# Odd attention in a two-model Trainium2 kernel: a head's scores by turns with the last head's transposes

## The chip, the cores and the metric

The kernel runs on one core of one Trainium2 chip. The metric is the device time of one execution in microseconds (us). Engines are named as the profile names them: PE is TensorE (its weight loads are PEld), DVE is VectorE, ACT is ScalarE, POOL is GpSimd, SP is SyncE. L194 is line 194 of the kernel before.

## The reference, cut to what matters

Two models run one after the other on 512 tokens of width 1024. The first has two layers of mixing and a feed-forward block. The second has an even layer and an odd layer, each with attention and a SwiGLU block. The change is in the odd layer's attention, and to a small part in the even layer's window attention. All arithmetic is float32; each operand of a large product is split into a high and a low part, and three products stand for one.

```python
def _odd_mixer(h, hc, w_in, w_out, q_g, k_g, rel_bias, ctx_out):
    q, k, v = split(h @ w_in)            # 16 heads of 64, q and k with an RMS norm
    qc, kc, vc = split(hc @ w_in)        # the same of 256 context tokens
    o = _neighbourhood_attention(q, k, v, kc, vc, rel_bias) @ w_out

def one_row(r):                          # of _neighbourhood_attention
    s_nb = jnp.einsum('bqhd,bjhd->bhqj', q_row, k_rows) * scale + bias[None]
    s_nb = jnp.where(mask[None, None], s_nb, NEG_2)
    s_cx = jnp.einsum('bqhd,bjhd->bhqj', q_row, k_ctx) * scale
    p = jax.nn.softmax(jnp.concatenate([s_nb, s_cx], axis=-1), axis=-1)
    return (jnp.einsum('bhqj,bjhd->bqhd', p[..., :n], v_rows)
            + jnp.einsum('bhqj,bjhd->bqhd', p[..., n:], v_ctx))
```

## The kernel before

One Python program writes straight-line code, with no loops left on the chip. A planner of the tile framework then lays down each engine's queue: it takes the instruction of highest priority, which is the one that the program wrote first, among those that its own costs hold ready and for whose output a buffer is free.

Odd attention (`odd`, L1403) handles its 16 heads in 4 groups of 4. `proj` (L1413) is the projection of one group to keys, queries and values. It is a generator: each step issues three matmuls of 256 columns and says what they take by the code's own count (0.33 us). `later` (L129) puts such a generator into a queue, `fill(us)` (L132) takes steps of it until `us` are used up, `drain` takes all the rest. During group `gr` the queue holds the projection of the next group, 128 steps or 42.2 us; during the last it holds three quarters of the out projection (`out_part`, L1437), 48 steps of 0.65 or 31.2 us. It ends each row block with a gate addition on DVE (`gate_add`, L1104).

A head has two stages. `s1` (L1483) loads the head's relative bias in three DMAs, subtracts it from the mask on POOL (L1492, L1494), and for each of 4 query blocks makes the scores (recorded as L438 and L439), adds the mask and takes the minimum on DVE (L443), and takes the exponential on ACT (L1508, L1514, L1516), whose running sums are added and inverted by DVE (L1520, L1521). A fill of 0.85 us follows each block. `s2` (L1524) calls `window_av` (L1022), which goes through 5 groups of blocks: PE transposes the exponentials into PSUM (L1030 for the two context groups, L1039 for the three window groups), ACT casts the high half and DVE subtracts for the low half (`split_r` and `split`, L176 and L177), a fill of 0.85 follows, and then PE adds the product with the values to `po` (L1034, L1048). At the end `fold` (L487) brings `po` to the output slab of the pair of heads, and one more fill follows.

The heads of a group go by `s1(1)`, `s2(0)`, `s1(2)`, `s2(1)` and so on: all four score blocks of a head, then all five groups of the head before. At the first head of each pair `stacks` (L1473) transposes queries and keys (L391) and writes them, scaled, to slabs (`stack`, L394: L407 on ACT, L411 and L413 on DVE). At the end of a pair `over_sums` (L495) spreads the 8 reciprocals of a token to 512 columns on POOL (L500), transposes that on PE (L504), multiplies on DVE (L506), and the pair's output is split for the out projection (`cat`).

Weights come by DMA into 4 raw buffers; ACT and DVE split them (`weight`, L164 and L165). Slabs of 2 KB per partition come from two pools in this stage, `F` with 18 and `R` with 23 slabs. Of PSUM's 8 banks 4 have the tag `A` (scores, transposes, `po`) and 4 the tag `G` (projections).

Of the kernel before, what the change touches and what calls it, by code (L numbers as in the profile page):

```python
# [10 lines left out]
F32R = mybir.dt.float32r  # L11
BF = mybir.dt.bfloat16
AF = mybir.ActivationFunctionType
# [27 lines left out]
OF = (0.85, 0.85, 0.85)  # L41
# [6 lines left out]
ODD = dict(F=18, R=23, L=4)  # L48
# [6 lines left out]
class Gen:  # L55
# [28 lines left out]
    def F(self, name, n=512):  # L84
        return self.tile("F", name, [128, 512])[:, :n]

    def R(self, name, n=512):
        return self.tile("R", name, [128, 512], F32R)[:, :n]
# [406 lines left out]
    def over_sums(self, y, rc, ident, view=None):  # L495

# [4 lines left out]
                                   rc.rearrange("p i e -> p (i e)")[:, :, None].to_broadcast([128, 2 * n, 64]))  # L501
        ps = self.P()[:, :n * 128]
# [519 lines left out]
    def window_av(self, es, ident, fill, vst, vctx):  # L1022
# [3 lines left out]
        hl, where = [], {}  # L1026
        for cb in range(2):
# [7 lines left out]
        for b, blocks in enumerate(self.WP):  # L1035
# [7 lines left out]
            self.fill(fill)  # L1043
            for kb in sorted({k for k, _ in blocks}):
                qs = [i for k, i in blocks if k == kb]
                o = blocks.index((kb, qs[0])) * 128
                for a, p in enumerate((h, l)):
                    nc.tensor.matmul(po[:, qs[0] * 128:qs[-1] * 128 + 128], vst[kb], p[:, o:o + len(qs) * 128],  # L1048
                                     start=False, stop=(b == 2 and a == 1))
        return po  # L1050
# [200 lines left out]
    def even(self, sc, sx, y):  # L1251
# [48 lines left out]
        def heads(z, scale, new, s1, s2, cat):  # L1300
            qs, ya, rc, prev = {}, {}, {}, None
            for h in range(9):
# [8 lines left out]
                if prev is not None:  # L1311
                    j = (h - 1) // 2
                    s2(h - 1, prev, ya[j])
                    if h % 2 == 0:
                        self.over_sums(ya[j], rc[j], self.ident)
# [45 lines left out]
        def s2(h, es, ya):  # L1361
            g = h // 4
            po = self.window_av(es, self.ident, EF[1], [v[:, g] for v in vst], [v[:, g] for v in vc])
            self.fold(ya, po, h % 2)
            self.fill(EF[2])
# [37 lines left out]
    def odd(self, sc, st):  # L1403
# [59 lines left out]

        new = lambda: ([], [], [])
        nxt = new()
        self.drain(proj(0, *nxt))
        for gr in range(4):
            zq, zk, vx = nxt
            nxt = new()
            self.later(proj(gr + 1, *nxt) if gr < 3 else out_part())  # L1470
            st_ = {}

            def stacks(hp):  # L1473
                qt = self.heads_t(zq, hp * 128, self.rident)
                q2 = [self.stack(qt, e, False, gcol[:, 0:1]) for e in range(2)]
                kt_ = self.heads_t(zk[2:], hp * 128)
                k2 = [self.stack(kt_, e, True, gcol[:, 1:2]) for e in range(2)]
                kt_ = self.heads_t(zk[:2], hp * 128)
                c2 = [self.stack(kt_, e, True, gcol[:, 1:2]) for e in range(2)]
                for e in range(2):  # L1480
                    st_[hp * 2 + e] = q2[e], k2[e], c2[e]

            def s1(hl, rc):  # L1483
                h = gr * 4 + hl
                qs, kx, kc = st_[hl]
                bias = self.small("nab", [128, 3, 256], bufs=2)
                src = t["od_rel_bias_2"][h]
                for v in range(3):
                    self.load(bias[:, v, :249], bass.AP(tensor=src.tensor, offset=src.offset + (16, 8, 0)[v],
# [330 lines left out]
```

## Time and profile before

| what | value |
|---|---|
| time, median of 3 runs | 3478.66 us (3477.15 to 3480.24) |
| the profiled execution's own time | 3484.61 us |
| its span, from the first to the last instruction | 3482.8 us |
| mean granted clock of PE | 0.993 |
| busy share of the span: PE, PEld, DVE, ACT, POOL | 98%, 84%, 63%, 45%, 8% |
| HBM traffic | 385.05 MB read, 16.88 MB written |

The profile shows one execution. A row of a group of instructions gives line, engine, operation, output and inputs, shapes, count, then busy time and mean duration, then the engine's idle time before them and what ended it. PE's matmuls overlap, so a single one's duration is longer than the step to the next. Odd attention's projection of the first group starts at about 2734 us, its heads run from 2776 to 3091 us, in four groups that begin near 2776, 2858, 2942 and 3024 us.

### The profile page before, as it was taken

How to read it: one execution, taken by the hardware profiler on the slowest of the kernel's cores; microseconds unless marked ns; L12 is line 12 of the kernel's file. 1: busy time of each engine (PE TensorE's matmuls, PEld its weight loads, DVE VectorE, ACT ScalarE, POOL GpSimd, SP SyncE). 2: the span in 40 equal slices, each digit the busy share in tenths (PEclk: the TensorE clock that was granted, in tenths of full speed). 3: DMA queues.
4: the chain of work that ended last, by engine and by line, in shares of the span. 5: the costliest groups of instructions: out<-in, count | busy, mean ns of one | idle time of the engine just before them, and what ended most of it. 6: DMA issues, size and time to landing. Idle time of an engine off the chain costs nothing.

```text
span 3482.8 us, 48256 instructions
## 1 busy us (share of the span) xinstructions
PE 3403.7 (98%) x18462; PEld 2938.1 (84%) x18462; DVE 2191.0 (63%) x3822; ACT 1560.6 (45%) x2933; POOL 276.4 (8%) x525
## 2 busy tenths in 40 slices
PE   9999999999999999999999999999999999989999
PEld 8888888888888888888887889888888888878887
DVE  5567646999564765579857777673334566673433
ACT  5545434424464553343434567553223466652222
POOL 2200000000031000000001100000000333300000
PEclk9999999999999999999999999999999999999999
DMA  4231234665323212446733133453333333233322
GB/s 127 84 91 55 76 106 153 204 220 176 111 76 107 67 61 85 144 151 218 252 121 129 61 121 126 145 189 121 97 97 120 81 57 62 66 110 112 97 91 85
DMA packets 144790, 405.06 MB, mean 116 GB/s; under 512 B 26768, under 2 KB 34992, under 8 KB 144560
## 3 DMA queue, kind: packets, MB, share of 16 engines
q1 hardware_dynamic: 144560, 401.99, 37.1%
q8 instruction: 145, 2.38, 0.3%
q14 instruction: 85, 0.70, 0.1%
HBM read 385.05 MB, written 16.88 MB: 115 GB/s over the span
## 4 chain that ended last, share of the span: by engine, by line
PE 82%; DVE 7%; ACT 5%; issue 3%; POOL 2%; DMA 1%; SPq 0%; DVEq 0%; ACTq 0%; POOLq 0%
PE ps L194 24%; PE ps L195 24%; PE ps L196 24%; PE ps L438 1%; PE ps L476 1%; PE ps L439 1%; PE ps L786 1%; DVE wl L165 1%; ACT stk L407 1%; PE ps L1048 1%; PE ps L302 1%; PE ps L1034 1%; PE ps L695 1%; DVE adaj L916 1%; ACT wh L164 1%
## 5 line engine op out<-in xcount | busy, mean ns | idle before, releaser
L164 ACT CAST wh<-wr 128x1024 fp32r<-128x1024 f32 (+2 forms) x540 | 557.3, 1032 | 1100.4 <-PE ps L195 491.0
L165 DVE TENSOR_TENSOR wl<-wr,wh 128x1024 fp32r<-128x1024 f32 (+2 forms) x540 | 649.9, 1204 | 578.4 <-ACT wh L164 571.9
L194 PE MATMUL ps<-xq,wh 128*128 128x512 f32 (+1 forms) x2664 | 952.4, 358 | 8.3 <-ACT xq L176 6.6
L195 PE MATMUL ps<-xq,wh 128*128 128x512 f32 (+1 forms) x2664 | 945.6, 355 | 1.0 <-DVE xq L177 0.9
L196 PE MATMUL ps<-xq,wl 128*128 128x512 f32 (+1 forms) x2664 | 944.7, 355 | 1.3 <-DVE wl L165 1.3
L194 PEld LDWEIGHTS ps<-xq,wh 128*128 128x128 f32 x2664 | 506.0, 190 | 73.8 <-ACT xq L176 8.5
L196 PEld LDWEIGHTS ps<-xq,wl 128*128 128x128 f32 x2664 | 506.0, 190 | 70.7 <-DVE wl L165 2.2
L195 PEld LDWEIGHTS ps<-xq,wh 128*128 128x128 f32 x2664 | 506.4, 190 | 64.9 <-DVE xq L177 1.9
L194 PE MATMUL ps<-wh,xq 128*128 128x256 f32 (+3 forms) x1056 | 341.7, 325 | 1.8 <-ACT wh L164 1.3
L196 PE MATMUL ps<-wh,xq 128*128 128x256 f32 (+3 forms) x1056 | 335.7, 319 | 0.7 <-DVE xq L177 0.7
L195 PE MATMUL ps<-wl,xq 128*128 128x256 f32 (+3 forms) x1056 | 336.3, 319 | 0.0
L194 PE MATMUL ps<-wh,hdh 128*128 128x512 f32 x704 | 274.3, 390 | 0.0
L196 PE MATMUL ps<-wh,hdl 128*128 128x512 f32 x704 | 274.2, 389 | 0.0
L195 PE MATMUL ps<-wl,hdh 128*128 128x512 f32 x704 | 274.0, 389 | 0.0
L194 PEld LDWEIGHTS ps<-wh,xq 128*128 128x128 f32 x1056 | 203.7, 193 | 9.9 <-ACT wh L164 1.8
L196 PEld LDWEIGHTS ps<-wh,xq 128*128 128x128 f32 x1056 | 203.4, 193 | 7.8 <-DVE xq L177 0.9
L195 PEld LDWEIGHTS ps<-wl,xq 128*128 128x128 f32 x1056 | 203.9, 193 | 6.4
L916 DVE SCALAR_TENSOR_TENSOR adaj<-adaw,cb 128x1024 bf16<-128x1024 f32 x160 | 194.7, 1217 | 17.3 <-DMA adaw<-in_ada_w_dram 16.6
L177 DVE TENSOR_TENSOR ptl<-ps,pth 128x512 fp32r<-128x512 f32 (+1 forms) x208 | 132.9, 653 | 51.4 <-ACT pth L176 50.0
L176 ACT CAST pth<-ps 128x512 fp32r<-128x512 f32 (+1 forms) x208 | 115.1, 573 | 93.3 <-PE ps L476 43.5
L195 PEld LDWEIGHTS ps<-wl,hdh 128*128 128x128 f32 x704 | 132.2, 188 | 27.4
L196 PEld LDWEIGHTS ps<-wh,hdl 128*128 128x128 f32 x704 | 132.1, 188 | 27.4
(434 smaller groups left out, 5250.7 us busy)
## 6 DMA issues: line engine op xcount, KB each, us to landing
wr<-in_ffn_w_gu_dram SPq DMA_DIRECT2D x132, 512.0 KB, 3.5
wr<-in_ffn_w_down_dram SPq DMA_DIRECT2D x110, 512.0 KB, 3.5
adaw<-in_ada_w_dram SPq DMA_DIRECT2D x96, 512.0 KB, 4.3
wr<-in_ffn_w_up_dram SPq DMA_DIRECT2D x88, 512.0 KB, 4.1
wr<-in_w_in_g_dram SPq DMA_DIRECT2D x48, 512.0 KB, 3.4
xd<-x SPq DMA_DIRECT2D x56, 256.0 KB, 2.0
x<-xd SPq DMA_DIRECT2D x56, 256.0 KB, 5.7
wr<-in_w_in_d_dram SPq DMA_DIRECT2D x32, 384.0 KB, 3.2
```

Source lines behind the costliest of these rows:

```text
L164: nc.scalar.copy(h, r)
L165: nc.vector.tensor_sub(l, r, raw(h))
L176: nc.scalar.copy(hi, src)
L177: nc.vector.tensor_sub(lo, src, raw(hi))
L194: mm(out, lh, rh, start=start, stop=False)
L195: mm(out, lh, rl, start=False, stop=False)
L196: mm(out, ll, rh, start=False, stop=stop)
L302: nc.tensor.transpose(ps[:, q * 128:q * 128 + 128], xn[hf][:, q * 128:q * 128 + 128], self.ident)
L407: nc.scalar.activation(dst, ps[own], AF.Copy, scale=scale[own])
L438: mm(out, q, k[0][:, ks], start=True, stop=False)
L439: mm(out, q, k[1][:, ks], start=False, stop=stop)
L916: nc.vector.scalar_tensor_tensor(j, w, 1.0, cb[s], op0=OP.mult, op1=OP.mult, accum_out=acc[s][:, m:m + 1])
```

## The change

It touches four places.

- A new function `weave` takes generators and runs them by turns, one step of each, with a fill after each step.
- `window_av` becomes such a generator. A group's value product is written only after the transposes of the group after it, and `fold` is called at its end (`done`). Even attention's `s2` runs it alone, with fills of 1.3 us, of which it had six before as well.
- `odd` runs all 16 heads in one loop. `s1` is a generator of four steps. Inside a group `weave` lets the last head's `window_av` and this head's `s1` take turns, beginning with `window_av`; the last head of a group runs its `window_av` alone, and the first head of a group its `s1` alone. Fills take 1.05 us in the first three groups and 0.8 us in the last. `stacks` of a pair stand ahead of the weave.
- The reciprocals are written by DVE straight into a slab of 512 columns, 256 elements for each head, through an input that repeats each of 4 sums 64 times; POOL's copy is left only in even attention (`spread`). In odd attention the pools `F` and `R` become one pool `S` of 41 slabs.

```diff
-OF = (0.85, 0.85, 0.85)
+OF = (1.05, 0.8)
...
-ODD = dict(F=18, R=23, L=4)
+ODD = dict(S=41, L=4)
...
+    def weave(self, gens, us):
+        gens = [g for g in gens if g is not None]
+        while gens:
+            for g in list(gens):
+                try:
+                    next(g)
+                except StopIteration:
+                    gens.remove(g)
+                else:
+                    self.fill(us)
...
-    def window_av(self, es, ident, fill, vst, vctx):
+    def window_av(self, es, ident, vst, vctx, done):
...
-            ph = self.split_r(p, "pt")
-            self.fill(fill)
-            for a in range(2):
-                nc.tensor.matmul(po, vctx[cb], ph[a], start=(cb == 0 and a == 0), stop=False)
+            ph = self.split_r(p, "pt")
+            def av():
+                for a in range(2):
+                    nc.tensor.matmul(po, vctx[cb], ph[a], start=(cb == 0 and a == 0), stop=False)
+            return av
...
+        for make, b in ((ctx, 0), (ctx, 1), (window, 0), (window, 1), (window, 2)):
+            av = make(b)
+            if last is not None:
+                last()
+            last = av
+            yield
+        last()
+        done(po)
+        yield
...
-                    self.fill(OF[0])
-                nc.vector.tensor_add(sums[:, :, 0], sums[:, :, 0], sums[:, :, 1])
-                nc.vector.reciprocal(rc[:, :, hl % 2], sums[:, :, 0])
-                return es
+                if i == NT - 1:
+                    nc.vector.tensor_add(sums[:, :, 0], sums[:, :, 0], sums[:, :, 1])
+                    nc.vector.reciprocal(rc.rearrange("p (i e d) -> p i e d", i=NT, e=2)[:, :, h % 2],
+                                         sums[:, :, 0:1].to_broadcast([128, NT, 64]))
+                yield
...
+        for h in range(17):
+            gr, hl = divmod(h, 4)
+            if h and hl == 0:
+                self.weave([av(h - 1)], OF[gr == 4])
+                over(h // 2 - 1)
+            if h < 16:
+                if hl == 0:
+                    self.drain()
+                    (zq, zk, vx), nxt = nxt, new()
+                    self.later(proj(gr + 1, *nxt) if gr < 3 else out_part())
+                if h % 2 == 0:
+                    stk[h], stk[h + 1] = stacks(zq, zk, hl // 2)
+                    y[h // 2] = self.F("ya")
+                    rc[h // 2] = self.F("rb")
+                es[h], vs[h] = [], vx
+                self.weave([av(h - 1) if hl else None, s1(h, stk.pop(h), rc[h // 2], es[h])], OF[gr == 3])
+                if hl == 2:
+                    over(h // 2 - 1)
```

## Rows read from the trace of the kernel before

**Rows 1.** The page, section 1: busy us, share of the span, instructions of PE.

```profile
PE 3403.7 (98%) x18462; PEld 2938.1 (84%) x18462; DVE 2191.0 (63%) x3822; ACT 1560.6 (45%) x2933; POOL 276.4 (8%) x525
```

**Rows 2.** Busy time by stretch: all heads of odd attention; their last group.

```profile
core 0: us, PE busy (x) PEld busy (x) DVE busy (x) ACT busy (x) POOL busy (x), PEclk, DMA share, GB/s
2776.00:3091.00 315.00, 296.87 (x2110) 268.06 (x2110) 214.26 (x391) 196.85 (x445) 94.60 (x156) 0.99 0.29 64
...
3024.00:3091.00 67.00, 62.78 (x345) 49.80 (x343) 53.89 (x102) 44.05 (x99) 7.56 (x19) 1.00 0.28 88
```

**Rows 3.** Who waited for whom, PE, 2734 to 3091: us in total, times, longest.

```profile
PE ps L1034 <- ACT pth L176: 6.2, 8, 1.5
PE ps L1034 <- DVE ptl L177: 4.6, 10, 0.9
PE ps L438 <- ACT stk L407: 3.1, 10, 0.4
PE ps L194 <- ACT cath L176: 2.1, 1, 2.1
PE ps L194 <- DVE gx L1106: 0.7, 1, 0.7
```

**Rows 4.** Timeline of PE near 2873: start, us, instruction, idle before and releaser.

```profile
2869.01 0.27 PE L1030 MATMUL ps<-rident,ew 128*128 128x128 f32 x1
...
2873.44 0.50 PE L1034 MATMUL ps<-pth,vs 128*128 128x512 f32 x1 [1.54 <-ACT pth L176]
...
2876.19 0.39 PE L1034 MATMUL ps<-ptl,vs 128*128 128x512 f32 x1
...
2877.94 0.49 PE L391 MATMUL ps<-rident,z 128*128 128x128 f32 x3
2878.24 0.44 PE L1048 MATMUL ps<-ptl,vs 128*128 128x384 f32 x1
```

**Rows 5.** Timeline of DVE, the same stretch.

```profile
2866.75 2.87 DVE L165 TENSOR_TENSOR wl<-wr,wh 128x1024 fp32r<-128x1024 f32 x1
...
2875.09 0.69 DVE L177 TENSOR_TENSOR ptl<-ps,pth 128x512 fp32r<-128x512 f32 x1 [0.43 <-ACT pth L176]
```

**Rows 6.** Timeline of POOL, the same stretch.

```profile
2866.32 2.21 POOL L1492 TENSOR_TENSOR nam<-namask,nab 128x744 f32<-128x744 f32 x1 [30.99 <-DVE onm L443]
```

**Rows 7.** Groups of DVE instructions by form, 2776 to 3091.

```profile
L165 DVE TENSOR_TENSOR wl<-wr,wh 128x1024 fp32r<-128x1024 f32 x24 | 32.6, 1357 | 8.6 <-ACT wh L164 8.6
L177 DVE TENSOR_TENSOR ptl<-ps,pth 128x512 fp32r<-128x512 f32 x48 | 32.1, 680 | 9.6 <-ACT pth L176 9.4
...
L1520 DVE TENSOR_TENSOR osum<-osum 128x4 f32<-128x4 f32 x16 | 13.6, 848 | 8.8 <-ACT ew L1508 8.8
```

**Rows 8.** Timeline of ACT, the stretch of rows 4.

```profile
2874.47 0.59 ACT L176 CAST pth<-ps 128x512 fp32r<-128x512 f32 x1 [1.08 <-PE ps L1030]
```

**Rows 9.** Timeline of PE at a pair's first scores.

```profile
2803.82 0.62 PE L438 MATMUL ps<-stk 128*128 128x256 f32 x3 [0.40 <-ACT stk L407]
```

**Rows 10.** Busy time by stretch, 2955 to 2965.

```profile
2955.00:2960.00 5.00, 3.26 (x18) 2.58 (x17) 2.92 (x5) 2.87 (x8) 2.76 (x7) 0.86 0.80 123
2960.00:2965.00 5.00, 5.00 (x35) 4.86 (x34) 2.39 (x5) 2.12 (x4) 0.00 (x0) 0.80 0.57 125
```

**Rows 11.** Who waited for whom, PE, even attention's window heads.

```profile
PE ps L1034 <- ACT pth L176: 0.6, 2, 0.4
```

**Rows 12.** Groups of DVE instructions by form, the whole span: reciprocals.

```profile
L1521 DVE RECIPROCAL orc<-osum 128x4 f32<-128x4 f32 x16 | 2.8, 176 | 0.4
L636 DVE RECIPROCAL drec<-dsum 128x8 f32<-128x8 f32 x8 | 1.6, 203 | 4.2 <-ACT ea L462 4.2
...
L758 DVE RECIPROCAL csm<-csm 128x16 f32<-128x16 f32 x4 | 1.0, 248 | 0.0
```

**Rows 13.** The copies of L500 in odd attention: duration min/median/max, first and last start.

```profile
L500 POOL COPY rb<-orc x8: 609/610/803, 2815.0 to 3084.2; 128x512 f32<-128x512 f32 x8
```

**Rows 14.** Who waited for whom, POOL, 2740 to 3090.

```profile
POOL ew L1512 <- PE ps L1039: 8.7, 4, 3.7
```

More of the change, by code (lines that the diff above doesn't have):

```diff
@@ L493, in fold, with spread @@
         nc.vector.tensor_add(y[own], y[own], v(po[own]))
-    def over_sums(self, y, rc, ident, view=None):
+    def spread(self, rc):
         n = rc.shape[1]
@@ L1020, with ctx @@
     WP = (((0, 0), (0, 1), (3, 2), (3, 3)), ((1, 0), (1, 1), (1, 2)), ((2, 1), (2, 2), (2, 3)))
-    def window_av(self, es, ident, fill, vst, vctx):
+    def window_av(self, es, ident, vst, vctx, done):
         nc = self.nc
         po = self.P()
-        hl, where = [], {}
-        for cb in range(2):
+        last = None
+        def ctx(cb):
             p = self.P()
@@ L1042, in window_av, with av @@
             self.split(ps[:, :n], h, l)
[L1043 to L1050, printed above, removed]
+            def av():
+                for kb in sorted({k for k, _ in blocks}):
+                    qs = [i for k, i in blocks if k == kb]
+                    o = blocks.index((kb, qs[0])) * 128
+                    for a, p in enumerate((h, l)):
+                        nc.tensor.matmul(po[:, qs[0] * 128:qs[-1] * 128 + 128], vst[kb], p[:, o:o + len(qs) * 128],
+                                         start=False, stop=(b == 2 and a == 1))
+            return av
+        for make, b in ((ctx, 0), (ctx, 1), (window, 0), (window, 1), (window, 2)):
[7 more added lines that the diff above has]
+        yield
     def fourier(self, ff, nt, dft, out):
@@ L1314, in heads @@
                     if h % 2 == 0:
-                        self.over_sums(ya[j], rc[j], self.ident)
+                        self.over_sums(ya[j], self.spread(rc[j]), self.ident)
                         if cat is not None:
@@ L1362, in s2 @@
             g = h // 4
-            po = self.window_av(es, self.ident, EF[1], [v[:, g] for v in vst], [v[:, g] for v in vc])
-            self.fold(ya, po, h % 2)
-            self.fill(EF[2])
+            self.weave([self.window_av(es, self.ident, [v[:, g] for v in vst], [v[:, g] for v in vc],
+                                       lambda po: self.fold(ya, po, h % 2))], EF[1])
         yx = self.xp.tile([128, 4, SEQ], F32, name="yx", tag="X", bufs=4)
@@ L1462, in odd, with stacks @@
         g, ws = [], []
+        def stacks(zq, zk, hp):
+            qt = self.heads_t(zq, hp * 128, self.rident)
+            q2 = [self.stack(qt, e, False, gcol[:, 0:1]) for e in range(2)]
+            kt_ = self.heads_t(zk[2:], hp * 128)
+            k2 = [self.stack(kt_, e, True, gcol[:, 1:2]) for e in range(2)]
+            kt_ = self.heads_t(zk[:2], hp * 128)
+            c2 = [self.stack(kt_, e, True, gcol[:, 1:2]) for e in range(2)]
+            return [(q2[e], k2[e], c2[e]) for e in range(2)]
@@ new lines, in s2, with over @@
+        def s2(h, es, vx, y):
+            hl = h % 4
+            return self.window_av(es, self.rident, [v[:, hl] for v in vx[2:]], [v[:, hl] for v in vx[:2]],
+                                  lambda po: self.fold(y.rearrange("p (r c) -> p r c", r=8), po, h % 2,
+                                                       lambda a: a.rearrange("p (c r) -> p r c", r=8)))
+        def over(j):
+            self.over_sums(y[j].rearrange("p (r c) -> p r c", r=8), rc[j], self.rident,
+                           lambda a: a.rearrange("p (c r) -> p r c", r=8))
+            cat[j] = self.split_r(y[j], "cat")
@@ L1546, in odd @@
+        self.drain()
         self.drain(out_end())
```

118 lines of the change are left out of this document (43 added, 75 removed).

## The prediction

> **What bounds the kernel now.** The page comes first: PE is busy for 98% of the span [rows 1]. So only PE's idle time, and time in which it runs at the lower clock, can be won. How much of that lies where the change works is in the table by stage [rows 2]: from 2776 to 3091 us, the heads of odd attention, PE is busy for 296.9 of 315.0 us and idles for 18.1; DVE has 214.3, so no other engine is short of time. PE's list of waits in that stage says what ended the idle time [rows 3]: 6.2 + 4.6 = 10.8 us (18 times) stand before the value products of a head's context groups (L1034), which wait for the two halves of their split, 3.1 us before scores that wait for their stack (L438), 2.1 us at the end of the stage, where the out projection waits for the last split, 0.7 us for a gate addition.
>
> Then the queues around one such wait are laid side by side. PE transposes at 2869.01 (L1030) and has the product of them only at 2873.44, after 1.54 us of idle time [rows 4]. ACT cast late because its last exponentials were late, and these because DVE's score minima stood behind a weight split (L165) of 2.87 us [rows 5], whose mean in the stage is 1.36 [rows 7]. POOL began its mask subtraction just before, at 2866.32, and ended it at 2868.53 [rows 6]; the split, begun at 2866.75, lasts about its usual time from there. The addition of a softmax's sums (L1520) is held in the same way: 848 ns on average for four elements [rows 7]. So the waits are delays of some 1.5 us in DVE and ACT, which a product placed shortly behind its transposes can't hide. [...]
>
> One more thing is to be seen in the rows: the queues don't follow the code's order. Three transposes of the next pair's heads (L391) stand ahead of the last value product of this head (2878.24), which the code has before them [rows 4]. The planner that writes the queues takes what it holds ready, by its own costs. An order by hand is a wish, and a wait shows where the planner's time and the chip's differ.
>
> **The change part by part.**
> *Value products a group later, scores between.* Before, a group's product came one fill (0.85 us of projection by the code's own count) behind its transposes. Undelayed, cast and low half take from 2874.47 [rows 8] to 2875.78 [rows 5], with the hand-overs 1.4 us. Now a fill, a score block, a fill and the next transposes come between. Three scores take 0.62 [rows 9] and three transposes 0.49 [rows 4], each with the time of the last to drain; I put a block at 0.5: 1.05 + 0.5 + 1.05 + 0.5 = 3.1 us. That is 1.7 more than the chain needs, and the longest wait is 1.5. Only the fourth head of each group runs alone (1.05 + 0.5, hardly more than the chain). I leave 2.0 of the 10.8 us: gain 8.8, between bounds of 0 and 10.8. A product behind a wait also takes 0.50 us in place of 0.39 [rows 4]; 18 x 0.11 = 2.0, of which the same share is 1.6.
>
> *First scores of a pair.* Within a group the last head's first transposes and one fill (1.5 us) now stand ahead of the scores that wait for a new stack. Of the ten waits for stacks six are of this kind, two in each of three groups, up to 0.40 us each [rows 3, 9], some 2 us together. I take half, 1.0; bounds 0 and 2.
>
> [...]
>
> *Even attention.* Its window heads get the later products too, at the same six fills of 1.3. Waits of L1034 for a cast there are 0.6 us [rows 11]: gain 0.5; bounds 0 and 0.6.
>
> *The reciprocals.* Before, DVE inverted four elements per head in 176 ns [rows 12], and POOL spread them, 8 copies of 0.61 us [rows 13]. Now DVE writes 256 elements per head, a size that the trace does not have: 4 elements take 176, 8 203, 16 248 ns [rows 12]. From 8 to 16 one costs 5.6 ns, which gives 248 + 240 x 5.6 = 1.6 us, so 1.42 more per head and 22.7 over 16 heads. The lower bound is a plain pass, half of the 0.68 us that 512 elements take [rows 7]; the upper has 6.75 ns each, as from 4 to 8 elements: 1.9 us. I take 1.6, by the slope of the longest. DVE then has 237 of the 315 us, and in the last group, which has the gate additions, 59.6 in place of 53.9 of 67 [rows 2]: under PE. What of it reaches PE? In this stage PE idled for 4.6 us on low halves [rows 3], while DVE spent 32.1 us on those of 512 columns and 13.6 on the additions ahead of them [rows 7]: 0.10 us for each. 22.7 x 0.10 = 2.3 us lost. The bounds are 0 and all of it (a rival). [...]
>
> The copies that go were hidden: PE's list has no wait for them [rows 3]. I count nothing; were one to stand in PE's way, it would be 0.61 us.
>
> *New nearness.* Heads 0, 4, 8 and 12 compute their scores without a partner, so their transposes start one fill (1.05 us) behind their last scores, and minimum and exponential aren't done by then. Where a consumer stands uncovered like that, before stacks, PE waits up to 0.40 us [rows 9], as the planner pulls other work up: 4 x 0.4 = 1.6 lost; bounds 0 and 4 x 1.54, the longest wait of the stage.
>
> *Fills and the pool.* A group has 40 fills of 0.85 = 34 us for 42.2 us of projection, the rest plain at its end; now 40 x 1.05 = 42. In the last group 31.2 us of out projection meet 40 x 0.8 = 32. PE's work is the same and only its pace changes: nothing, while PE is full. The one pool has the same 41 slabs, but a pair's reciprocals now hold one, and splits overlap by two. That costs nothing in groups 0 to 2; for the last it is a rival.
>
> **Sum.** 8.8 + 1.6 + 1.0 + 1.7 + 0.5 - 2.3 - 1.6 = 9.7 us less. The profiled execution took 3484.6 us, 1.8 of it outside its span of 3482.8, and would take 3474.9. It lies 5.9 above the median of the runs, 3478.7, from which the same 9.7 give **3469.0**. A difference of under 0.2% (7.0 us) is about what a measurement of this kernel can't tell from none.
>
> **The rivals.**
> *The waits move (same).* The holds between DVE and POOL stay, and the planner had spread the queues already; then the products have room, but transposes and scores stand as short behind late exponentials as the products did, and the change does little of what it says. For it: what is held all stays [rows 5 to 7]. Against: transposes now start some 4 us behind their head's last scores, except in four heads. Clock and even attention would still give 2 to 3 us: 3476.
>
> *VectorE's queue in front of PE (slower).* At a head's end the addition waits for the last exponential and perhaps for POOL, then the reciprocal holds DVE for 1.6 us; behind both stand the low half of the last transposes and the next head's minima. The last product comes one product and one fill behind, 1.4 us, just the chain. If all of the 1.42 reaches PE at every head, 22.7 go against 12.0 of gain without it: 10.7 more, 3489. From 0.75 us per head there is no gain, from 1.19 it is slower by 0.2%. Against: the planner can put that product behind the next head's work, and DVE keeps a quarter of its time.
>
> *All idle time goes (faster).* Only the tail's 2.1, the gate addition's 0.7 and 1.2 us of scores stay of the 18.1; with restarts, clock and even attention 14.1 + 2.0 + 1.7 + 0.5 = 18.3: 3460. It needs that every hold is hidden.
>
> *Slabs run short in the last group (same).* There 12 splits of finished pairs, 6 of values, 5 of stacks, 10 of exponentials, 4 of products and 4 of outputs and reciprocals make 41, and the out projection wants 4 to 8 for x. Four memsets of new exponentials already wait for a slab that transposes still read, 8.7 us in total, on POOL [rows 14]. If each of 8 gate additions then costs PE the 0.7 us that one of them did, 5.6 of the 9.7 go: 3475.
>
> **How the numbers follow.** My forecast has a chance of 0.45, its own range 3464 to 3473; all idle time gone 0.15; the waits move 0.24; slabs short 0.05; VectorE's queue 0.11. The range reaches from just above the best case well into the way to the slower one, 3461 to 3484, and leaves out some 0.04 below and 0.15 above. Faster by over 0.2% is 0.40 of the forecast's chance and the best case: 0.55. Within it lie 0.05 of the forecast, most of the moved waits and of the slabs: 0.30. Slower, 0.15, is VectorE's queue and the worst of those two.
>
> **What would show it.** In the changed profile: waits of the context product under 3 us in the stage; PE idle there for about 10 us; no stretch at the lower clock in the third group; 16 reciprocals of about 1.6 us on DVE, 8 copies fewer on POOL; DVE some 22 us busier. I am wrong if PE's list of waits shows as much under transposes, scores or the last product as it lost under the first, or if the stage is shorter by much less than 10 us although that list is short.

## The result: 22 us slower

The changed kernel took 3501.6 us (median of 4 runs, 3499.3 to 3504.5) beside 3479.5 of the kernel before (4 runs, 3477.2 to 3481.5) on the same chip: a ratio of 1.0061, 95% interval 1.0048 to 1.0074. The forecast of 3469.0 and its range to 3484 are wrong, and so is the sign. A difference of 22 us is three times what this kernel's measurement leaves open.

Lines of the changed kernel are 12 to 24 higher: the context product L1034 is L1054, the window product L1048 is L1072, the transposes L1030 are L1049, scores L438 are L450, the addition of sums L1520 is L1540, the reciprocal L1521 is L1541. Of the helpers, the cast L176 is L188, the low half L177 is L189, the weight split L165 is L177, the stack L407 is L419, the out projection's product L194 is L206, and POOL's subtraction L1492 is L1513. Kernels with `rb` in a tile of its own have a few more lines (the context product is L1057 in the changed order and L1037 in the old one).

The page's first section of the changed kernel, beside [rows 1]:

```profile
PE 3405.1 (97%) x18462; PEld 2941.5 (84%) x18462; DVE 2221.9 (63%) x3822; ACT 1562.3 (45%) x2933; POOL 277.5 (8%) x517
```

PE is as busy as before, so the time is idle time. Busy time by stretch says where. Each stretch is one group of heads, from the first transposes of its stacks to those of the next group; the last one ends with the first transposes behind the stage. The columns are those of [rows 2]. First the kernel before:

```profile
2769.90:2851.50 81.60, 77.71 (x599) 72.76 (x598) 52.92 (x95) 52.00 (x116) 28.52 (x47) 1.00 0.32 65
2851.50:2934.70 83.20, 78.00 (x599) 72.89 (x598) 54.08 (x97) 51.16 (x117) 29.28 (x45) 1.00 0.30 58
2934.70:3019.10 84.40, 79.20 (x598) 74.19 (x597) 54.20 (x97) 51.15 (x118) 29.24 (x45) 0.98 0.28 57
3019.10:3100.80 81.70, 77.48 (x406) 61.63 (x405) 64.32 (x119) 50.14 (x114) 8.70 (x21) 0.98 0.28 91
```

The changed kernel:

```profile
2768.30:2850.10 81.80, 76.62 (x599) 73.06 (x598) 58.37 (x93) 50.63 (x112) 27.94 (x45) 1.00 0.32 65
2850.10:2936.40 86.30, 78.33 (x599) 74.34 (x598) 61.81 (x97) 51.86 (x117) 29.53 (x43) 0.98 0.28 55
2936.40:3024.20 87.80, 80.06 (x598) 75.55 (x597) 61.87 (x98) 51.44 (x116) 29.64 (x43) 0.96 0.28 55
3024.20:3118.30 94.10, 80.08 (x398) 62.51 (x397) 72.97 (x121) 50.78 (x116) 9.00 (x21) 0.93 0.24 79
```

The stage takes 350.0 in place of 330.9 us. Of the 19.1 us 12.4 lie in the last group, and the clock falls from group to group, 1.00 to 0.93. Who waited for whom on PE, 2776 to 3118, beside [rows 3]:

```profile
PE ps L450 <- ACT stk L419: 8.7, 8, 2.0
PE ps L1072 <- DVE ptl L189: 8.7, 9, 2.4
PE ps L1049 <- DVE ya L505: 5.7, 4, 1.5
PE ps L1054 <- DVE ptl L189: 4.6, 5, 1.6
PE ps L206 <- ACT cath L188: 3.6, 1, 3.6
...
PE ps L1054 <- ACT pth L188: 0.4, 1, 0.4
```

The casts in front of the context product are gone (6.2 to 0.4), as forecast. The low halves stay and now stand under the window products too (8.7 us, none before), and two more waits have grown or come: 8.7 us for stacks (3.1 before) and 5.7 us (none before) for the fold of a head's output (`ya`), which frees the bank that the next transposes want. All of them end at DVE or at ACT, whose stacks waited for DVE about as long as before (11.2 us, 11.7 before). What DVE has more of stands in its groups by form in the stage:

```profile
L1541 DVE RECIPROCAL rb<-osum 128x256 f32<-128x256 f32 x16 | 28.0, 1750 | 0.5
...
L1540 DVE TENSOR_TENSOR osum<-osum 128x4 f32<-128x4 f32 x16 | 15.5, 972 | 8.5 <-ACT ew L1528 8.5
```

The reciprocal takes 1750 ns (forecast 1.6 us). The addition of four elements takes 972 on average, 157 at the least and 2105 at the most. DVE's timeline around the wait of PE at 2873.58 puts the two in a row:

```profile
2868.67 2.04 DVE L1540 TENSOR_TENSOR osum<-osum 128x4 f32<-128x4 f32 x1
2870.63 0.68 DVE L455 CUSTOM_DVE_ANT_0 ps<-ps,nam 128x512 f32<-128x512 f32 x1
2871.24 0.13 DVE L455 DVE_READ_ACCUMULATOR2_ANT onm<- 128x1 f32 x1
2871.24 1.74 DVE L1541 RECIPROCAL rb<-osum 128x256 f32<-128x256 f32 x1
2872.91 1.22 DVE L189 TENSOR_TENSOR ptl<-ps,pth 128x512 fp32r<-128x512 f32 x2
```

POOL in the same stretch, and PE:

```profile
2867.65 3.03 POOL L1513 TENSOR_TENSOR nam<-namask,nab 128x744 f32<-128x744 f32 x1 [24.01 <-DVE onm L455]
```

```profile
2870.05 0.40 PE L1054 MATMUL ps<-pth,vs 128*128 128x512 f32 x1
...
2873.58 0.50 PE L1054 MATMUL ps<-ptl,vs 128*128 128x512 f32 x1 [1.58 <-DVE ptl L189]
```

The addition begins while POOL subtracts and ends with it; a minimum and the reciprocal follow; the low half, due behind its cast, begins 2.9 us after the product of that cast (2870.05), and PE waits 1.58 us. That is the place which the rival of VectorE's queue named. It explains the waits for low halves; that it explains those for stacks isn't shown. Two more parts of the change may have done as much: one pool in place of two, and the order itself. Three theories were therefore tried: **A**, the reciprocal and the held addition in front of PE; **B**, the order; **C**, the one pool.

### The profile page after: what moved, and what is told of

Its sections match the earlier page's. It is cut to its first block, busy times and chain, and to the rows that moved or that the text cites. A ratio compares the mean times of both kernels' runs of the same rounds, so it can differ in the third digit from the quotient of the medians.

```text
span 3501.6 us, 48185 instructions
## 1 busy us (share of the span) xinstructions
PE 3405.1 (97%) x18462; PEld 2941.5 (84%) x18462; DVE 2221.9 (63%) x3822; ACT 1562.3 (45%) x2933; POOL 277.5 (8%) x517
## 4 chain that ended last, share of the span: by engine, by line
PE 84%; DVE 7%; ACT 4%; issue 3%; POOL 1%; DMA 1%; SPq 0%; DVEq 0%; ACTq 0%; POOLq 0%
PE ps L206 24%; PE ps L207 24%; PE ps L208 24%; PE ps L450 2%; PE ps L451 1%; DVE wl L177 1%; PE ps L488 1%; PE ps L803 1%; ACT stk L419 1%; PE ps L314 1%; PE ps L1072 1%; ACT wh L176 1%; PE ps L1054 1%; PE ps L712 1%; PE ps L1062 1%
## 5 line engine op out<-in xcount | busy, mean ns | idle before, releaser
L176 ACT CAST wh<-wr 128x1024 fp32r<-128x1024 f32 (+2 forms) x540 | 557.3, 1032 | 1099.0 <-PE ps L207 482.8
L177 DVE TENSOR_TENSOR wl<-wr,wh 128x1024 fp32r<-128x1024 f32 (+2 forms) x540 | 652.8, 1209 | 570.5 <-ACT wh L176 563.5
L206 PE MATMUL ps<-xq,wh 128*128 128x512 f32 (+1 forms) x2664 | 952.1, 358 | 8.6 <-ACT xq L188 6.6
L206 PEld LDWEIGHTS ps<-xq,wh 128*128 128x128 f32 x2664 | 506.0, 190 | 74.3 <-ACT xq L188 8.6
L206 PE MATMUL ps<-wh,xq 128*128 128x256 f32 (+3 forms) x1056 | 340.2, 323 | 2.2 <-ACT wh L176 1.3
L206 PE MATMUL ps<-wh,hdh 128*128 128x512 f32 x704 | 274.3, 390 | 0.0
L206 PEld LDWEIGHTS ps<-wh,xq 128*128 128x128 f32 x1056 | 202.4, 192 | 11.0 <-ACT wh L176 1.8
L189 DVE TENSOR_TENSOR ptl<-ps,pth 128x512 fp32r<-128x512 f32 (+1 forms) x208 | 133.6, 651 | 46.9 <-ACT pth L188 44.2
L206 PEld LDWEIGHTS ps<-wh,hdh 128*128 128x128 f32 x704 | 132.2, 188 | 27.4
```

The source lines that it names most:

```text
L176: nc.scalar.copy(h, r)
L177: nc.vector.tensor_sub(l, r, raw(h))
L189: nc.vector.tensor_sub(lo, src, raw(hi))
L206: mm(out, lh, rh, start=start, stop=False)
```

## The experiments

The kernel before took 3480.6 to 3482.4 us (medians) beside these runs; ratios are to it, with their 95% intervals. The runs come from four chips; between runs of different paragraphs a difference of some 2 us may be that of the chips.

**One part alone.** The first four kernels undo or do one part. `weave_small_recip` is the change with four-element reciprocals that POOL spreads, as before; `before_one_pool` is the kernel before with only the pool changed; `before_spread_recip` adds the long reciprocals to that; `weave_sum_by_reduce` is the change with the sums added by a reduction of one input in place of an addition of two. The diffs here and below show the main lines alone, shortened.

```diff
 weave_small_recip, to the changed kernel:
-nc.vector.reciprocal(rc.rearrange("p (i e d) -> p i e d", i=NT, e=2)[:, :, h % 2],
-                     sums[:, :, 0:1].to_broadcast([128, NT, 64]))
+nc.vector.reciprocal(rc[:, :, h % 2], sums[:, :, 0])
...
-self.over_sums(y[j].rearrange("p (r c) -> p r c", r=8), rc[j], self.rident,
+self.over_sums(y[j].rearrange("p (r c) -> p r c", r=8), self.spread(rc[j]), self.rident,
 weave_sum_by_reduce, to the changed kernel:
-nc.vector.tensor_add(sums[:, :, 0], sums[:, :, 0], sums[:, :, 1])
+nc.vector.tensor_reduce(tot, sums, axis=AX.X, op=OP.add)
 before_one_pool, to the kernel before (before_spread_recip: long reciprocals too):
-ODD = dict(F=18, R=23, L=4)
+ODD = dict(S=41, L=4)
```

`weave_small_recip`. 

> The changed kernel with its reciprocals as before: VectorE inverts 4 sums a head, GpSimd spreads them. Scores by turns, late products and the one pool stay. Theory A (VectorE's queue: the 1.75 us reciprocal, behind an addition that GpSimd holds, delays the low halves, the fold and the stacks that PE waits for): most of the 22 us comes back, 3472 to 3482. Theory B (the new order itself puts transposes and scores too near to what they need): under a third comes back, 3494 or more.

`weave_sum_by_reduce`. 

> The changed kernel with the addition of a head's sums, which reads two SBUF inputs, made as a reduction, which reads one; the long reciprocal stays. Theory A1 (the hold by GpSimd's mask subtraction matters as much as the reciprocal): the sums' instruction falls from 970 to some 170 ns on average, 16 x 0.8 = 13 us less of VectorE, and 6 to 12 us of time come back, 3490 to 3496. Theory A2 (the reciprocal alone matters): 3499 or more. Theory B: no change, 3501.

`before_spread_recip`. 

> The kernel before with the spread reciprocals on VectorE and the one pool, but its old order. Theory A: the same 25 us more of VectorE delay the products here too, 10 to 20 us slower than before, 3489 to 3499. Theory B: the reciprocal is not what costs, within 3 us of before, 3476 to 3482.

`before_one_pool`. 

> The kernel before with the one pool of 41 slabs alone. Theory A and B: within 2 us of before, 3477 to 3481. A third theory, C (slabs shared by all tiles cost waits): 3 us or more slower.

Measured: `weave_small_recip` 3502.4 (1.0058, 1.0043 to 1.0073), `weave_sum_by_reduce` 3496.0 (1.0039, 1.0024 to 1.0054), `before_spread_recip` 3506.2 (1.0074, 1.0057 to 1.0090), `before_one_pool` 3501.9 (1.0056, 1.0041 to 1.0071). The reduction in the changed kernel gave back 5.6 us. `weave_small_recip` answers little by itself: with the short reciprocals POOL's copy comes back too. The surprise is the last run: the pool alone, which the prediction costed at nothing, loses 20 us. PE's waits of `before_one_pool`, 2734 to 3110:

```profile
PE ps L504 <- POOL rb L500: 14.5, 3, 4.8
PE ps L1034 <- ACT pth L176: 5.8, 5, 1.5
```

Its timeline of POOL shows the copy behind three chains of root and scaling:

```profile
2812.68 1.05 POOL L992 TENSOR_TENSOR z<-z,hrms 128x512 f32<-128x512 f32 x1
...
2815.81 1.04 POOL L992 TENSOR_TENSOR z<-z,hrms 128x512 f32<-128x512 f32 x1
...
2818.93 1.04 POOL L992 TENSOR_TENSOR z<-z,hrms 128x512 f32<-128x512 f32 x1
2819.91 0.61 POOL L500 COPY rb<-orc 128x512 f32<-128x512 f32 x1
```

Before, the first copy started at 2815.0 [rows 13], behind one such chain. The planner takes an instruction up only when a slab for its output is free; in the shared pool the copy's came free later, and PE, whose transposes of the copy stand in its queue, waited 4.8 us. `weave_small_recip` has the same three waits, 13.9 us. The changed kernel has no such copy and must lose its time in another way.

**Two pools, and the copy's own tile.** `one_pool_rb_own` is `before_one_pool` with one slab less and the spread reciprocals in a tile of their own; the other three keep the changed order with two pools.

```diff
 weave_two_pools (to weave_small_recip), weave_two_pools_spread (to the changed kernel):
-ODD = dict(S=41, L=4)
+ODD = dict(F=17, R=24, L=4)
 weave_two_pools_reduce: weave_two_pools with the tensor_reduce above
 one_pool_rb_own, to before_one_pool (S=40):
-rb = self.F("rb")
+rb = self.small("rb", [128, 512], bufs=1)
```

`weave_two_pools`. 

> The changed order (scores by turns with the last head's transposes, value products a group later), but with two pools of slabs again (17 and 24) and the reciprocals of four elements spread by POOL, as before the change. Theory C (the loss is the single pool's: it alone cost 20 us in before_one_pool, and the order with short reciprocals on that pool cost the same 20): with two pools the order is worth what it takes off the waits, so 3465 to 3482, and TensorE's three long waits of the over-sums transposes for POOL's copy (14.5 us in before_one_pool, 13.9 in weave_small_recip) are gone. Theory B (the order itself costs, and hides a gain of the pool under it): over 3492. Theory A (VectorE's long reciprocal): gone here as well, so it can't be told from C by this run alone; weave_two_pools_spread does that.

`weave_two_pools_spread`. 

> The change as it is, but for two pools (17 and 24) in place of one of 41. Theory C: the long reciprocals cost 16 x 1.57 us of VectorE but little of TensorE, so within 5 us of weave_two_pools, and faster than the changed kernel by 15 us or more (3470 to 3487). Theory A (the reciprocal and the sums' addition in front of TensorE): about 10 to 25 us over weave_two_pools, waits of the window products for low halves of 8 us or more, as the changed kernel has them. If the pool does not matter beside the reciprocal: 3495 to 3503, as the changed kernel.

`weave_two_pools_reduce`. 

> weave_two_pools with the addition of a softmax's two sums (two SBUF inputs) as a tensor_reduce (one input) into a tile of its own. In weave_sum_by_reduce the same edit gave back some 5 us beside the changed kernel. Theory A's part that the addition is held by POOL: 3 to 6 us faster than weave_two_pools, VectorE's additions fall from about 0.9 us to under 0.3 each. If the held addition was only in front of TensorE together with the long reciprocal behind it: within 2 us of weave_two_pools.

`one_pool_rb_own`. 

> The kernel before with one pool, of 40 slabs, and the spread reciprocals (POOL's copy) in a tile of their own, so that the copy never waits for a slab of the pool. Theory C in its narrow form (the copy's slab comes free too late in the one pool and TensorE's over-sums transposes wait for it, 14.5 us in three waits): the three waits go and the time falls by some 12 to 15 us below before_one_pool, to 3485 to 3491. C in its wide form (in one pool any tile's slab may come free late, whichever it is): another wait takes their place and the time stays at 3495 to 3505. If the single pool costs by what the planner does with the order of all slabs and not by waits: idle time stays about as before and the loss is in the clock.

Measured: 3497.8 (1.0049, 1.0034 to 1.0064), 3489.8 (1.0027, 1.0014 to 1.0039), 3487.8 (1.0016, 1.0006 to 1.0025), 3482.5 (1.0008, 0.9999 to 1.0017). Theory C holds in its narrow form for the old order: with a tile of its own the copy starts at 2789.1, no wait for it is left, and the single pool costs nothing measurable. It missed for the changed order: in a pool of 17 the copy's slab was as late as in the one of 41. `weave_two_pools_reduce` shows it as its one large loss, 2690 to 3150:

```profile
PE ps L521 <- POOL rb L511: 14.0, 3, 5.2
...
PE ps L450 <- ACT stk L419: 4.2, 8, 2.0
```

Not one wait of a window product for a low half is on its list: the reduction, 160 ns on average, took them away, and 9.9 us of time. And with the long reciprocals two pools give back 11.8 us, though the window products still wait 7.0 us for low halves there.

**Put together.** `weave_rb_own` has the changed order, short reciprocals, one pool of 40 and the copy's own tile; with `_reduce` the sums by reduction. `change_two_pools_reduce` has the long reciprocals, two pools and the reduction. `before_reduce` is the kernel before with the reduction alone.

```diff
 weave_rb_own, to weave_small_recip: S=40 and rb as in one_pool_rb_own
 weave_rb_own_reduce, change_two_pools_reduce, before_reduce:
-nc.vector.tensor_add(sums[:, :, 0], sums[:, :, 0], sums[:, :, 1])
+nc.vector.tensor_reduce(tot, sums, axis=AX.X, op=OP.add)
```

`weave_rb_own`. 

> The changed order with the reciprocals as before the change (four elements, spread by POOL) and the spread ones in a tile of their own beside a pool of 40 slabs. weave_small_recip is the same but for that tile; it took 3502 and TensorE waited 13.9 us in three waits for POOL's copy. Theory C (the copy's late slab is what cost the old order 20 us, and the changed order with short reciprocals too): the three waits go and the time falls by 12 to 18 us, to 3483 to 3490 or less; what it then stands below one_pool_rb_own (3482.5) is what the order itself gains, between 0 and 12 us. Theory B (the order itself costs): over 3494, with waits for stacks or exponentials in place of those for the copy.

`weave_rb_own_reduce`. 

> weave_rb_own with the addition of a softmax's two sums as a tensor_reduce with one input. By weave_two_pools_reduce (3487.8, whose TensorE waits in the stage are three for POOL's copy, 14.0 us, and little else: the low halves' waits under 1 us): with the copy's wait gone too, 3471 to 3477, the fastest of all so far, below the kernel before by 5 us or more. If the waits of the copy only move to another tile of the pool: 3482 to 3490.

`change_two_pools_reduce`. 

> The change with its long reciprocals, but with two pools (17 and 24) and the sums by tensor_reduce: what is left against the kernel before is the order and the reciprocals. The two edits gave back 12 us (weave_two_pools_spread) and 5.6 us (weave_sum_by_reduce) one at a time. If they add up: 3483 to 3486. If the held addition and the pool delay the same products: 3487 to 3490. Compared with weave_rb_own_reduce it shows what the long reciprocals alone cost: by theory A 8 us or more; if they are under TensorE's work, under 4 us.

`before_reduce`. 

> The kernel before with nothing changed but the addition of a softmax's two sums, as a tensor_reduce with one input. If the held addition stands in front of TensorE in the old order as well (848 ns on average, 13.6 us in all on VectorE, and the low halves behind it waited for 4.6 us): 2 to 5 us faster than before, waits of the context product for low halves under 3 us. If it is hidden there, and only the changed order brings it to the path: within 2 us of before.

Measured: 3486.3 (1.0015, 1.0005 to 1.0024), 3475.0 (0.9981, 0.9972 to 0.9991), 3476.4 (0.9985, 0.9976 to 0.9994), 3476.6 (0.9985, 0.9975 to 0.9994). The reduction is worth 11.3 us in the changed order with short reciprocals and 5.1 in the old one. `change_two_pools_reduce` fell by 13.4 (from `weave_two_pools_spread`), further than either forecast allowed, and stands 1.4 above `weave_rb_own_reduce`: with two pools and short additions the long reciprocals cost PE next to nothing (`weave_split_rb_own_reduce` below, the same with short ones, took 3475.6), although DVE still spends 28.0 us on them.

**What is left: the pool's size, and the order.** Two runs change the slabs of the changed kernel; two compare the orders with all else put right (16 and 24 slabs, the copy's own tile, the reduction).

```diff
 change_pool_42, to the changed kernel:
-ODD = dict(S=41, L=4)
+ODD = dict(S=42, L=4)
 change_rb_pair_own, to the changed kernel (S=39):
-rc[h // 2] = self.F("rb")
+rc[h // 2] = self.small("rbp", [128, 512], bufs=2)
 weave_split_rb_own_reduce, to weave_rb_own_reduce; before_split_rb_own_reduce, old order:
-ODD = dict(S=40, L=4)
+ODD = dict(F=16, R=24, O=1, L=4)      # O=1: rb in its own tile
```

`change_pool_42`. 

> The changed kernel with 42 slabs in its one pool in place of 41, nothing else. The changed kernel itself took 3501.6. If the 12 us that two pools give back are a shortage of slabs (the pairs' reciprocals hold one each, so tiles come free too late): one slab more gives back a part, 4 us or more, 3490 to 3497. If it is the order that a shared pool brings, whatever its size: 3499 to 3503.

`change_rb_pair_own`. 

> The changed kernel with the reciprocals of a pair in two tiles of their own and 39 slabs in the pool, so as much memory as before. If the reciprocals' slabs were the late ones, as POOL's copy was in the old order: 3487 to 3493, as with two pools. If the stacks and exponentials are short of slabs: no better, 3499 to 3506 (there are two less for them than now, one of which a pair's reciprocals held for most of the time).

`weave_split_rb_own_reduce`. 

> The changed order with short reciprocals, sums by tensor_reduce, the spread reciprocals in a tile of their own and two pools (16 and 24): everything put right that the runs so far showed to cost. weave_rb_own_reduce took 3475.0 with 6.1 us of waits for stacks, most of it in the last group, where change_two_pools_reduce had 1.8. If two pools end those: 3469 to 3473. If its last group is short of slabs in another way: 3474 to 3478.

`before_split_rb_own_reduce`. 

> The same as weave_split_rb_own_reduce in the old order (scores a head ahead of the transposes, value products one fill behind theirs). before_reduce took 3476.6. If the order is worth what it takes off the waits of the value products for their casts (6.2 us in before_reduce): 3474 to 3478, 4 to 6 us above weave_split_rb_own_reduce. If the order is worth nothing once the additions are short: within 2 us of it.

Measured: 3500.8 (1.0055, 1.0042 to 1.0069), 3502.8 (1.0056, 1.0040 to 1.0071), 3475.6 (0.9980, 0.9971 to 0.9989), 3473.9 (0.9977, 0.9967 to 0.9987). So one slab more, or two tiles for the reciprocals, gives nothing back of the 12 us that the long reciprocals lose in one pool, and the order as a whole is worth nothing that the measurement shows. By groups, though, the two orders differ. `weave_split_rb_own_reduce`:

```profile
2765.20:2843.60 78.40, 75.58 (x599) 72.78 (x598) 50.69 (x93) 50.89 (x112) 27.32 (x47) 1.00 0.35 67
2843.60:2922.60 79.00, 76.54 (x598) 73.05 (x597) 52.24 (x97) 52.12 (x117) 28.01 (x45) 1.00 0.32 60
2922.60:3000.10 77.50, 76.31 (x598) 73.08 (x597) 51.40 (x99) 51.97 (x116) 29.89 (x45) 1.00 0.33 62
3000.10:3087.70 87.60, 80.02 (x407) 63.33 (x406) 65.46 (x122) 51.86 (x116) 9.29 (x21) 0.94 0.26 83
```

`before_split_rb_own_reduce`:

```profile
2768.70:2848.20 79.50, 77.00 (x599) 72.82 (x598) 50.55 (x95) 51.95 (x116) 28.34 (x47) 1.00 0.34 67
...
2929.30:3010.50 81.20, 77.33 (x599) 72.87 (x598) 51.54 (x98) 51.22 (x118) 29.05 (x45) 1.00 0.30 59
3010.50:3089.30 78.80, 75.47 (x406) 60.84 (x405) 62.85 (x119) 50.30 (x113) 8.60 (x21) 1.00 0.29 94
```

The changed order is 1.1, 2.1 and 3.7 us shorter in the first three groups (78.4, 79.0, 77.5 beside 79.5, 81.1, 81.2) and 8.8 longer in the last, with nearly the same instructions there (407 and 406 products of PE). Each figure is of one profiled execution; the run below that keeps this order in the first three groups repeats them to 0.1 us. The stretch in which the last group loses it, `weave_split_rb_own_reduce` by 10 us:

```profile
3030.00:3040.00 10.00, 6.52 (x28) 4.87 (x28) 6.81 (x11) 7.00 (x13) 0.24 (x2) 0.83 0.34 105
3040.00:3050.00 10.00, 10.00 (x43) 8.21 (x42) 5.85 (x11) 2.48 (x7) 0.00 (x0) 0.83 0.08 26
```

PE, waiting 2.0 us for a stack and 1.5 for the low half of one, is busy for 6.5 of 10 us and then works 10 us at a mean granted clock of 0.83.

**The last group alone.** `weave_but_last_group` takes the old order there; `before_wide_fills` keeps the old order throughout but fills 1.05 in the first three groups.

```diff
 weave_but_last_group, to weave_split_rb_own_reduce (OF = (1.05, 0.85); window_av: late=h < 12):
-self.weave([av(h - 1) if hl else None, s1(h, stk.pop(h), rc[h // 2], es[h])], OF[gr == 3])
+turns = [av(h - 1) if hl else None, s1(h, stk.pop(h), rc[h // 2], es[h])]
+for gens in ([turns] if gr < 3 else [turns[1:], turns[:1]]):
+    self.weave(gens, OF[gr == 3])
 before_wide_fills, to before_split_rb_own_reduce:
-OF = (0.85, 0.85, 0.85)
+OF = ((1.05, 1.05, 1.05), (0.85, 0.85, 0.85))     # the second in the last group
```

`weave_but_last_group`. 

> weave_split_rb_own_reduce with the old order in the last group alone: scores of a head, then the last head's transposes with each product one fill of 0.85 behind. That kernel took 3475.6, the old order throughout 3473.9. If the last group is where the order loses: its stretch falls from 89 us to 79 to 81, the first three stay at 76 to 80, and the time is 3464 to 3469, the fastest of all. If the loss comes from the hand-over between groups or the order's first three groups only lend time from the last: 3472 to 3476.

`before_wide_fills`. 

> before_split_rb_own_reduce (3473.9) with fills of 1.05 in place of 0.85 in the first three groups, the old order kept. If the gain of the changed order in groups 0 to 2 is that of the wider fills (the products of a group stand 0.2 us of projection further from their transposes, and no plain projection is left for the end of a group): 3465 to 3470, groups of 77 to 79 us. If it is that of the later products and of the scores between: within 2 us of 3474, with the context product's waits for casts, up to 1.5 us, as before.

Measured: 3470.4 (0.9970, 0.9959 to 0.9981), the fastest median of all, and 3476.4 (0.9987, 0.9979 to 0.9996). The first lies between the two ranges that were expected of it, the second 0.4 us above the upper of its own, so neither pair of readings holds as a whole. `weave_but_last_group`, first and last group:

```profile
2767.60:2845.90 78.30, 75.51 (x597) 72.70 (x596) 50.54 (x93) 50.89 (x112) 27.34 (x47) 1.00 0.35 68
...
3002.50:3085.40 82.90, 76.36 (x406) 60.74 (x405) 65.87 (x122) 51.28 (x116) 9.60 (x21) 1.00 0.27 89
```

`before_wide_fills`, the same:

```profile
2772.70:2852.10 79.40, 77.03 (x598) 72.56 (x597) 49.23 (x93) 51.18 (x112) 27.87 (x47) 1.00 0.34 67
...
3011.70:3094.50 82.80, 76.30 (x405) 60.71 (x404) 65.75 (x122) 51.23 (x116) 9.55 (x21) 1.00 0.28 89
```

The old order in the last group, with fills of 0.85 in place of 0.8 there, gives back 4.7 of the 8.8 us (87.6 to 82.9) and the full clock. The other 4 go with the wide fills of the groups ahead, in either order (82.9 and 82.8 beside 78.8): the last group's forecast of 79 to 81 missed by them. Of the 6.9 us that the changed order gains in the first three groups (234.9 beside 241.8) the wide fills alone bring 2.8 (239.0), the later products and turns 4.1. PE's waits of the context product for casts show the fills' part too, 2690 to 3150, first in `before_split_rb_own_reduce`, then in `before_wide_fills`:

```profile
PE ps L1037 <- ACT pth L176: 5.7, 5, 1.5
PE ps L1037 <- ACT pth L176: 1.3, 1, 1.3
```

The one wait that is left lies in the last group: fills of 1.05 alone, without the later products, take those of the first three groups away. `weave_but_last_group` lies 10 us under the kernel before; against `before_split_rb_own_reduce` its intervals overlap.

## Why the prediction was wrong, by its steps

**"Fills and the pool", the step that failed.** It had two halves. The pool "costs nothing in groups 0 to 2": in the old order it alone cost 20 us by POOL's late copy, shown by `one_pool_rb_own`. In the changed kernel the copy is gone and the pool costs 11.8 us (`weave_two_pools_spread`), or 19.6 where the additions are short (`weave_sum_by_reduce`, `change_two_pools_reduce`); by the groups' starts the first three groups are 11.4 us longer (255.9 us in the changed kernel, 244.5 there; the two profiled executions differ by 16.7 in all). One place of it is seen in the changed kernel's timeline of DVE, before PE's 1.54 us for `ya` at 2824.34:

```profile
2818.12 1.75 DVE L1541 RECIPROCAL rb<-osum 128x256 f32<-128x256 f32 x1
2819.79 0.49 DVE L189 TENSOR_TENSOR ptl<-ps,pth 128x384 fp32r<-128x384 f32 x1
2820.77 2.80 DVE L177 TENSOR_TENSOR wl<-wr,wh 128x1024 fp32r<-128x1024 f32 x1 [0.48 <-ACT wh L176]
2823.60 0.69 DVE L505 TENSOR_TENSOR ya<-ya,ps 64x512 f32<-64x512 f32 x1
```

The fold stands behind a reciprocal and a weight split of 2.80 us. In `weave_two_pools_spread`, which differs by the pool alone, it runs directly behind the reciprocal:

```profile
2811.57 1.75 DVE L1541 RECIPROCAL rb<-osum 128x256 f32<-128x256 f32 x1
2813.36 0.69 DVE L505 TENSOR_TENSOR ya<-ya,ps 64x512 f32<-64x512 f32 x1
```

In `weave_sum_by_reduce`, which keeps the one pool, the fold stands behind a weight split of 2.77 us as in the changed kernel, and PE waits 1.5 us for it. So at this place the pool acts through the order that the planner lays down; that the rest of the 11.8 us comes about in the same way isn't shown. Why one pool and long reciprocals together give the worse order stays open; a slab more and the reciprocals' own tiles did not change it, and with short reciprocals one pool costs nothing (`weave_rb_own_reduce` 3475.0, `weave_split_rb_own_reduce` 3475.6). The second half, "PE's work is the same and only its pace changes", failed in the last group: 8.8 us there in the kernels put right, order and fills about half each. Why the wide fills reach into it isn't settled.

**"The reciprocals": the price right, the company wrong.** 1.75 us lies between the 1.6 taken and the upper bound of 1.9. With two pools and short additions the long ones cost PE about 1 us (2.3 forecast; the intervals overlap). With one pool they cost far more: 15 us in the changed order (`weave_rb_own` 3486.3, the changed kernel 3501.6), 24 in the old (`one_pool_rb_own`, `before_spread_recip`). Theory A, a queue that only grows, doesn't explain that: the same 28 us of DVE are harmless in another order.

**The held addition, not in the sum.** The prediction named the hold and let it stay at no cost. It was already worth 5.1 us before. In the changed order it was worth 9.9 to 13.4 in three kernels, and 5.6 in the changed kernel itself, where the one pool stood beside it. It is the mis-sized part of "value products a group later": 2.0 us were left for all the waits that a later product can't hide, and 13.7 were measured under the context and window products of the changed kernel (4.6, 0.4 and 8.7; 10.8 before), a loss of 2.9 where 8.8 were to be gained. In the changed kernel ten of the 16 additions lay for 0.88 us or more beside POOL's subtraction (L1513) or scaling (L1009) and took 0.90 to 2.10 us; the other six took 0.16 or 0.17. The one-input reciprocal took 1734 to 1754 ns in all 16, among them one (2836.54) that ran beside the subtraction for 1.67 us, and the one-input reduction took a mean of 160 (`change_two_pools_reduce`).

**"First scores of a pair" and "new nearness".** The first was to gain 1.0 us; waits for stacks rose from 3.1 to 8.7, nearly half of them in the last group (4.1). They are 6.1 in `weave_rb_own_reduce`, which has neither long reciprocals nor held additions, so the order itself makes part of them. The second was to lose 1.6 where transposes stand close behind their exponentials; that wait is 0.3 us. The transposes wait 5.7 us for the fold instead. Waits under transposes, scores and the last products were the prediction's own sign of being wrong.

**What was right, and what was luck.** The waits for casts did go (6.2 to 0.4), but wider fills would have done most of it in the old order. With the hold and the late copy gone, waits under the context product are 1.8 us in `weave_rb_own_reduce` (10.8 before); that the 9.0 removed are close to the 8.8 of the sum is luck, as the reduction alone takes the 4.6 for low halves away in the old order (`before_reduce`). The gain in the first three groups is real. No run shows the 1.7 us that the sum takes for the clock, and the changed kernel went the other way: its mean granted clock was 0.96 in the third group and 0.93 in the last (0.98 in both before), with PE idle for 14.0 us of the last (4.2 before). Even attention's waits for casts stayed at 0.6 us [rows 11]. Of the rivals VectorE's queue had the sign and one of the places. Its price, 3489, was too low and its cause only a part: with two pools and short additions the same reciprocals cost next to nothing.

The account of the 22 us, by the runs: the pool and the additions together make up all of it, within the measurement. Without both, the changed kernel is where the old one is with the reduction (`change_two_pools_reduce` and `before_reduce` are equal), so order and reciprocals then cost nothing that the measurement shows. How it divides depends on which goes first. Two pools first give back 11.8, the reduction then 13.4; the reduction first gives back 5.6 (`weave_sum_by_reduce`), two pools then 19.6. Of the additions' part 5.1 us were in the kernel before as well. So the pool is 12 to 20 of the 22 us, and what the change adds to the cost of the held additions is 8 down to about nothing: the two delay the same work in part.

## What to carry to other kernels

Before several edits are costed as one, each that changes buffers is worth a price of its own: a pool's size may stay while the planner's order, and so who stands behind whom on a helper engine, changes, at a cost of up to 20 us here. Look first for short instructions that last long (four elements in 848 ns): replacing that addition took 5 us off the old kernel with one line. And a reordering is judged stage by stage: this one gains 7 us in the groups with plenty of independent work and loses 9 in the last. Used in part it gave the lowest time, 3470.4, though not clear of the old order with the same repairs, 3473.9.

## What the hardware showed unexpectedly

A subtraction on POOL and a two-input instruction on DVE both lasted longer where they ran side by side here. Beside the weight split of 2.80 us shown above (1.23 at 2851.35, with no subtraction on POOL) POOL's subtraction of 24 columns took 1.25 us, and 0.25 at 2870.64:

```profile
2822.42 1.25 POOL L1515 TENSOR_TENSOR nam<-namask,nab 128x24 f32<-128x24 f32 x1
```

In the changed kernel's last group PE was busy for 4.23 of 10 us; the mean granted clock was 0.81 in that stretch and 0.68 in the next (0.50 from 3062 to 3070), and 1.00 again after that. Stretches of 10 us:

```profile
3054.00:3064.00 10.00, 4.23 (x19) 2.90 (x19) 6.66 (x8) 4.40 (x9) 2.18 (x2) 0.81 0.33 106
3064.00:3074.00 10.00, 8.13 (x37) 6.90 (x38) 6.69 (x13) 6.39 (x15) 0.34 (x4) 0.68 0.06 20
3074.00:3084.00 10.00, 10.00 (x57) 8.27 (x55) 9.12 (x16) 4.28 (x10) 0.61 (x6) 1.00 0.11 35
```
